# Order of the latent passes of a shared-key attention layer, the last row's store and second square, and the place of the conditioning sums in the heads

## The chip, the cores and the metric

The kernel runs on one core of a Trainium2 chip. The metric is the device time of one execution in microseconds, from the median of several runs. A profiled execution gives, beside its own time, the instructions of each engine in order of time: TensorE (PE, its weight loads PEld), VectorE (DVE), ScalarE (ACT), GpSimd (POOL) and SyncE (SP, which only issues transfers here; ScalarE issues some too).

## What is computed

A trunk of two layers over a sequence of 1024 rows of width 1024, float32. Layer 0 has a gated short convolution and a squared-ReLU MLP. Behind it, one shared key and value side is built from the residual stream, and layer 1 attends to it. This is the part that the change touches:

```python
def shared_kv(x, c_act, kv_ada_w, kv_ada_b, kv_norm_g, kv_a_w, kv_a_norm_g, kv_b_w, cos, sin):
    shift, scale = jnp.split(c_act @ kv_ada_w + kv_ada_b, 2, axis=-1)
    hkv = modulate(rmsnorm(x, kv_norm_g), shift, scale)
    kv_a = hkv @ kv_a_w                                    # 1024 x (256 + 64)
    c_kv = rmsnorm(kv_a[..., :KV_LORA], kv_a_norm_g)       # key latent, 256
    k_pe = apply_rope(kv_a[..., KV_LORA:], cos, sin)       # rotary key, 64
    kv = (c_kv @ kv_b_w).reshape(B, S, N_HEADS, QK_NOPE + V_HEAD)
    return kv[..., :QK_NOPE], kv[..., QK_NOPE:], k_pe

def mla_mixer(h, q_a_w, q_a_norm_g, q_b_w, o_w, k_nope, v, k_pe, cos, sin):
    q = (rmsnorm(h @ q_a_w, q_a_norm_g) @ q_b_w)           # query latent, 384; 8 heads of 128 + 64
    ...                                                    # scores, mask, softmax, values, output
```

The query side reads `h = modulate(rmsnorm(x, norm_g[1, 0]), ...)` with layer 1's own shift and scale ("1m"), the key side the same normalized rows with another shift and scale ("kv").

## The kernel before

Every float32 product is three matmuls (line 156): both operands are split into a high part and the rest (`hi`, `lo`), and low times high, high times low and high times high are summed in one PSUM bank. A high part is written by ScalarE or VectorE, a low part by VectorE (lines 159 and 160, 436 to 442). The sequence is held in two halves of 512 rows, "half 0" (row tiles 0 to 3) and "half 1" (row tiles 4 to 7).

`down_pairs` ends layer 0's MLP. Its last four row tiles go one after another: late products (L790), then `Seam.tile`, then `seam.front` of one step. `Seam.tile` adds the products, takes the sum of squares on ScalarE (`squares`, L271 and L273), scales and adds the row to the residual on VectorE (L327, L328), issues the row's store to `xs` from ScalarE (L329), and takes a second sum of squares, that of the new residual row. `Seam.flush` later turns it into the normalized row `y` (L278 on VectorE, L311 on ScalarE). The normalized rows are what the latents read.

A *step* of `h_steps` makes one of the eight column blocks of `h` for one half: four transposes on TensorE (L433) into a bank (`room`, mostly one of two `tp` banks), an eviction with scale and shift on ScalarE (L436, into one of two `tt` tiles), and on VectorE a cast for the high part (L441) and a subtraction for the low part (L442). Where `twice` is set, ScalarE writes the high part too. `front` issues a step's transposes and evictions, `back` the VectorE part.

The latents are eight passes over `h`, each pass 24 matmuls of 128x512 per 128 output columns. Before the change their order is: query latent of half 0 (three passes, `first_latents`; the third makes the columns of "1m", half 1), query of half 1 (the third makes "kv", half 0, in the place of "1m", half 0), key latent of half 0 (two passes; the second makes "kv", half 1), rotary key of half 0, key of half 1, rotary key of half 1. `latent` evicts each pass (L1193), squares it (L1194), sums (L1196), and then at once sums over partitions with a matmul by ones (L1197), takes the root (L1198), a reciprocal of 512 elements per partition (L1199), scales (L1201) and splits (L1202, L1203). The three query weight tiles are split once and kept for both halves; `up_split` has three buffers.

Heads 0 to 7 follow. Before the loop, head 0's query, rotary query and key are projected, half 1 first. Each head computes scores for row tiles 7 down to 0 and interleaves projections of the next head. `run_bg(5)` in each head does five steps of the conditioning sums (`ada_bc`, `ada_fm`; 34 steps in all, 24 of them a scaled sum on VectorE, nearly all on L186, with a 512 KB load each). Head 0 also makes the four value tiles, two after scores 7 and two after scores 6.

What sets the order: the instructions of a block inside `pinned()` keep their written order on each engine; all others are ordered by a planner that places an instruction where it expects its inputs and engine to be free. Transfers from SP go in the order that the planner gave. Buffers of a tag are reused as their last readers end, so a weight tile or a raw tile (four buffers) that is kept longer holds back a load.

Of the kernel before, what the change touches and what calls it, by code (L numbers as in the profile page):

```python
# [17 lines left out]
P = 128  # L18
D = 1024
S = 1024  # L20
KD = D // P
# [27 lines left out]
def trunk_kernel(ctx: ExitStack, tc: tile.TileContext, x, c, ada_w, ada_b, norm_g, conv_in_w, conv_w,  # L49
# [63 lines left out]
    def ld(out_, in_):  # L113
        nc.sync.dma_start(out_, in_)
# [169 lines left out]
    class Seam:  # L284
# [23 lines left out]
        def flush(self):  # L308
            if self.rest is not None:
                y, xr, ss = self.rest  # L310
                nc.scalar.activation(y, xr, AF.Copy, scale=rroot(ss))  # L311
            self.rest = None

        def tile(self, t, add, steps):
# [4 lines left out]
            with pinned():  # L319
# [251 lines left out]
    def first_latents(seam, steps, ws, h):  # L571

        ps_ = []
        for m, w in enumerate(ws):
            p_ = mm_ps() if m else big_ps()[:, :HALF]
            for k in range(KD):
                with pinned():
                    mm(p_, (w[0][:, k, :], w[1][:, k, :]), (h[0][:, k, :], h[1][:, k, :]), k == 0, k == KD - 1)
                    if m == 0 and k == 0:
                        seam.flush()  # L580
                    elif m == 2:
                        seam.back()
                        seam.front(steps, 1)
            ps_.append(p_)
# [73 lines left out]
    def down_pairs(ys, wd, before, seam, key=None, preps=()):  # L658
# [67 lines left out]
        with pinned([mybir.EngineType.SP]):  # L726
# [451 lines left out]
    firsts = first_latents(seam, h_steps(tp, ys, 1, "1m", hs[1]), ws, hs[0])  # L1178
# [4 lines left out]
    def latent(h, hf, ws, g, dst, steps=None, firsts=None):  # L1183
# [5 lines left out]
        rs = sqs[0]  # L1189
        sp = tp_ps()  # L1190
# [6 lines left out]
        nc.tensor.matmul(sp, ones, sqs[0], start=True, stop=True)  # L1197
        nc.scalar.activation(rs, sp, AF.Sqrt, scale=1.0 / (n * P), bias=eps_1)  # L1198
        nc.vector.reciprocal(rs, rs)  # L1199
        for m in range(n):  # L1200
            nc.vector.scalar_tensor_tensor(raws[m], raws[m], g[:, m:m + 1], rs, op0=ALU.mult, op1=ALU.mult)  # L1201
            nc.scalar.activation(dst[0][:, m, sl], raws[m], AF.Copy)  # L1202
            nc.vector.tensor_tensor(dst[1][:, m, sl], raws[m], dst[0][:, m, sl].bitcast(F32), op=ALU.subtract)  # L1203
# [28 lines left out]
    def rotary_keys(hf):  # L1232
        sl = slice(hf * HALF, (hf + 1) * HALF)
        z, y = halves(row_tile())
        rotated(up_mm(wk, hk[hf]), hf, 1.0, stab, z, y)
# [357 lines left out]
```

## Time and profile before

| | us |
|---|---|
| median of 3 runs | 2160.37 (2159.45 to 2161.99) |
| profiled execution, its own time | 2159.2 |
| its span, first to last instruction | 2157.4 |
| TensorE busy | 2062.0 (96%) |
| VectorE busy | 1541.2 (71%) |
| ScalarE busy | 1084.3 (50%) |

The mean granted TensorE clock is 0.991 of full speed. In the rows below, an instruction's row holds its start, its duration, engine and line, operation, output and input tiles, shapes, and in brackets how long its engine stood idle before it and what it waited for. A row of a stage holds its length, then the busy time and the number of instructions of PE, PEld, DVE, ACT and POOL, the granted clock, the share of the DMA engines and GB/s; where the view is of one line, only that line's engine is in it. A row of a group holds the count, total busy time and mean ns, and the idle time before it. Matmuls are pipelined, so the distance between starts, not the duration of one, tells their pace.

### The profile page before, as it was taken

What the parts mean: (1) busy time and instruction counts of PE and PEld (TensorE: products, weight loads), DVE (VectorE), ACT (ScalarE), POOL (GpSimd) and SP (SyncE); (2) the same over time, 40 slices, a digit from 0 to 9 for tenths busy, and PEclk for the clock granted to TensorE, in tenths of its full rate; (3) what the DMA queues carried; (4) which work ended last, traced back from release to release, by engine and by line L of the source; (5) the groups of instructions that cost most, each with busy time, mean ns of one, the idle gap of its engine ahead of it and who ended that gap; (6) DMA issues with size and microseconds to landing.
All of it is one profiled execution on the core that took longest, in us unless ns stands there. A gap on an engine that the chain in (4) does not pass through costs nothing.

```text
span 2157.4 us, 25064 instructions
## 1 busy us (share of the span) xinstructions
PE 2062.0 (96%) x9438; PEld 1688.2 (78%) x9438; DVE 1541.2 (71%) x2087; ACT 1084.3 (50%) x1533; POOL 5.3 (0%) x13
## 2 busy tenths in 40 slices
PE   4999999989999999999899999999899999999998
PEld 3788878768888788888677788887678888788886
DVE  6877876876665669977688887756875665566576
ACT  4533353745554444455665565555744444544443
POOL 0000000000000000000000000000000000000000
PEclk9999999999999999999999999999999999999999
DMA  7444464254553889656223331143254653774355
GB/s 223 121 138 147 137 205 133 88 184 161 182 181 139 280 292 322 208 166 211 69 70 120 97 96 35 59 135 138 71 185 150 215 180 134 266 252 158 98 175 167
DMA packets 251023, 344.47 MB, mean 160 GB/s; under 512 B 19253, under 2 KB 142482, under 8 KB 250902
## 3 DMA queue, kind: packets, MB, share of 16 engines
q1 hardware_dynamic: 208408, 252.50, 37.4%
q10 hardware_dynamic: 42494, 90.38, 11.3%
q8 instruction: 74, 1.21, 0.2%
q14 instruction: 47, 0.39, 0.1%
HBM read 258.94 MB, written 83.89 MB: 159 GB/s over the span
## 4 chain that ended last, share of the span: by engine, by line
PE 77%; DVE 11%; ACT 6%; DMA 3%; issue 2%; ACTq 0%; SPq 0%; DVEq 0%
PE one L156 42%; PE mm L156 20%; PE tp L156 7%; PE big L156 3%; PE big L1360 2%; ACT junk L271 2%; DVE y L327 1%; PE tp L1386 1%; DVE raw L328 1%; DMA aw<-in_ada_w_dram 1%; ACT slot L1210 1%; DVE av L909 1%; PE tp L433 1%; DVE ring L160 1%; DVE acc L186 1%
## 5 line engine op out<-in xcount | busy, mean ns | idle before, releaser
L156 PE MATMUL one<-slot,uphi 128*128 128x512 f32 x1224 | 377.8, 389 | 0.0
L156 PEld LDWEIGHTS one<-slot,uphi 128*128 128x128 f32 x1224 | 230.4, 188 | 48.3 <-issue 0.5
L156 PE MATMUL one<-ring,ring 128*128 128x512 f32 x1152 | 262.9, 389 | 2.3 <-DVE ring L160 2.3
L160 DVE TENSOR_TENSOR uplo<-raw,uphi 128x1024 fp32r<-128x1024 f32 x127 | 153.3, 1222 | 143.1 <-ACT uphi L159 143.1
L156 PEld LDWEIGHTS one<-ring,ring 128*128 128x128 f32 x1152 | 215.9, 188 | 48.3 <-ACT ring L159 3.1
L156 PE MATMUL one<-slot,uplo 128*128 128x512 f32 x612 | 240.7, 393 | 8.2 <-DVE y L528 3.8
L160 DVE TENSOR_TENSOR ring<-raw,ring 128x1024 fp32r<-128x1024 f32 x144 | 174.3, 1220 | 55.6 <-ACT ring L159 55.3
L159 ACT ACTIVATE ring<-raw 128x1024 fp32r<-128x1024 f32 x144 | 149.5, 1052 | 106.6 <-DMA raw<-ha 61.6
L159 ACT ACTIVATE uphi<-raw 128x1024 fp32r<-128x1024 f32 x127 | 134.7, 1061 | 118.6 <-PE one L156 82.3
L156 PE MATMUL mm<-ring,ring 128*128 128x512 f32 x768 | 185.0, 390 | 1.6 <-DVE ring L160 1.6
L156 PE MATMUL tp<-ring,ring 128*128 128x512 f32 x768 | 183.9, 389 | 0.0
L159 ACT ACTIVATE ring<-w 128x1024 fp32r<-128x1024 f32 x80 | 84.8, 1060 | 178.7 <-PE tp L156 102.7
L156 PEld LDWEIGHTS mm<-ring,ring 128*128 128x128 f32 x768 | 143.7, 188 | 32.1 <-DVE ring L160 2.5
L156 PEld LDWEIGHTS tp<-ring,ring 128*128 128x128 f32 x768 | 144.1, 188 | 29.9
L160 DVE TENSOR_TENSOR ring<-w,ring 128x1024 fp32r<-128x1024 f32 x80 | 97.8, 1222 | 81.1 <-ACT ring L159 81.1
L156 PEld LDWEIGHTS one<-slot,uplo 128*128 128x128 f32 x612 | 115.2, 188 | 35.8 <-DVE y L528 5.5
L186 DVE SCALAR_TENSOR_TENSOR acc<-raw,csil,acc 128x1024 f32<-128x1024 f32 x88 | 112.5, 1278 | 22.8 <-DMA raw<-in_ada_w_dram 18.0
L526 ACT ACTIVATE y<-one 128x512 f32<-128x512 f32 x66 | 39.0, 591 | 159.6 <-PE one L156 118.5
L156 PE MATMUL mm<-slot,uphi 128*128 128x512 f32 x344 | 109.2, 399 | 9.6 <-DVE slot L398 9.4
L156 PE MATMUL one<-slot,s 128*128 128x512 f32 x468 | 112.9, 390 | 1.1 <-DVE s L160 1.1
L156 PEld LDWEIGHTS one<-slot,s 128*128 128x128 f32 x468 | 87.6, 188 | 20.6 <-DVE s L160 2.4
L156 PE MATMUL one<-q,uphi 128*128 128x512 f32 x328 | 101.9, 392 | 0.0
(267 smaller groups left out, 3614.4 us busy)
## 6 DMA issues: line engine op xcount, KB each, us to landing
ha<-y ACTq DMA_DIRECT2D x224, 256.0 KB, 4.0
raw<-ha SPq DMA_DIRECT2D x112, 512.0 KB, 4.0
raw<-in_ada_w_dram SPq DMA_DIRECT2D x80, 512.0 KB, 4.3
raw<-in_mlp_up_w_dram SPq DMA_DIRECT2D x70, 512.0 KB, 4.5
w<-in_mlp_down_w_dram SPq DMA_DIRECT2D x48, 512.0 KB, 7.0
raw<-in_mlp_down_w_dram SPq DMA_DIRECT2D x32, 512.0 KB, 4.0
raw<-in_conv_in_w_dram SPq DMA_DIRECT2D x18, 512.0 KB, 4.1
xs<-raw ACTq DMA_DIRECT2D x18, 512.0 KB, 2.8
```

The costliest lines, as they stand in the source:

```text
L156: nc.tensor.matmul(out_, lhs[a], rhs[b], start=first and i == 0, stop=last and i == 2, skip_group_check=more)
L159: nc.scalar.activation(hi, src, AF.Copy)
L160: nc.vector.tensor_tensor(lo, src, hi.bitcast(F32), op=ALU.subtract)
L186: nc.vector.scalar_tensor_tensor(acc, raw, s, acc, op0=ALU.mult, op1=ALU.add)
L271: nc.scalar.activation(junk, src, AF.Square, accum_out=ss)
L327: nc.vector.scalar_tensor_tensor(y, y, rroot(ss), self.gmb, op0=ALU.mult, op1=ALU.mult)
L328: nc.vector.tensor_tensor(xr, xr, y, op=ALU.add)
L433: nc.tensor.transpose(p_[:, t * P:(t + 1) * P], ys[half * 4 + t][:, k * P:(k + 1) * P], ident)
L526: nc.scalar.activation(dst, x_, AF.Copy)
L909: nc.vector.scalar_tensor_tensor(acc, raw[:, i, :], csil[:, i:i + 1], acc, op0=ALU.mult, op1=ALU.add)
L1210: nc.scalar.activation(y[32 * i:32 * i + 32, :], p_[32 * j:32 * j + 32, :], AF.Copy, scale=scale)
L1360: nc.tensor.matmul(o_, a, m_, start=j == 0, stop=j == 4)
```

## The change

The diff does five things.

1. In the last row tiles of `down_pairs`, the step (transposes and evictions) is issued before the row's tile, not after it.
2. For the last row tile (`held`), the store and the second sum of squares are not issued in `Seam.tile` but in `flush`, which now stands in the third pass of the first latent, in the middle of its eight steps.
3. `first_latents`: its first pass reads the low parts of `h` two groups later than the high parts. Its third pass makes "kv", half 0.
4. The passes: query 0, key 0, rotary key 0 (makes "kv", half 1), key 1, rotary key 1 (makes "1m", half 1), query 1. `latent` returns its end (sum over partitions, root, reciprocal, scaling, split), which is called later. The query weights are loaded and split a second time for half 1. The sine table is held in a row tile.
5. Head 0: keys of both halves first, then query and rotary query of half 0, two value tiles, then query and rotary query of half 1; the other two value tiles follow scores 7 and 6. `run_bg(6)` in heads 1 to 7, none in head 0.

```diff
         def flush(self):
             if self.rest is not None:
-                y, xr, ss = self.rest
-                nc.scalar.activation(y, xr, AF.Copy, scale=rroot(ss))
+                y, xr, ss, held = self.rest
+                nc.scalar.activation(y, xr, AF.Copy, scale=rroot(ss or squares(self.nx, xr)))
+                if held is not None:
+                    nc.scalar.dma_start(self.xdst[held * P:(held + 1) * P, :], xr)
             self.rest = None
...
-                nc.scalar.dma_start(self.xdst[t * P:(t + 1) * P, :], xr)
+                if not held:
+                    nc.scalar.dma_start(self.xdst[t * P:(t + 1) * P, :], xr)
                 if not self.last:
-                    self.rest = (y, xr, squares(self.nx, xr))
+                    self.rest = (y, xr, None, t) if held else (y, xr, squares(self.nx, xr), None)
...
+            ps_.append(p_)
+            if m == 0:
+                jobs = []
+                for k in range(KD + LAG):
+                    jobs += [(1, 0, k), (0, 0, k)] * (k < KD) + [(0, 1, k - LAG)] * (k >= LAG)
+                with pinned():
+                    for i, (a, b, k) in enumerate(jobs):
+                        nc.tensor.matmul(p_, w[a][:, k, :], h[b][:, k, :], start=i == 0, stop=i == len(jobs) - 1)
+                    seam.back()
+                continue
             for k in range(KD):
                 with pinned():
                     mm(p_, (w[0][:, k, :], w[1][:, k, :]), (h[0][:, k, :], h[1][:, k, :]), k == 0, k == KD - 1)
-                    if m == 0 and k == 0:
-                        seam.flush()
-                    elif m == 2:
+                    if m == 2:
                         seam.back()
                         seam.front(steps, 1)
-            ps_.append(p_)
+                        if k == KD // 2:
+                            seam.flush()
...
-                    seam.tile(4 + t, lambda: done(t, banks_[t]), [])
                     with pinned():
+                        seam.back()
                         seam.front(steps, 1)
+                    seam.tile(4 + t, lambda: done(t, banks_[t]), [], t == 3 and bool(key))
...
-    firsts = first_latents(seam, h_steps(tp, ys, 1, "1m", hs[1]), ws, hs[0])
+    firsts = first_latents(seam, h_steps(tp, ys, 0, "kv", hs[0]), ws, hs[0])
...
-    latent(hs[0], 0, ws, gq, qaT, firsts=firsts)
-    steps = h_steps(tp, ys, 0, "kv", hk[0])
-    latent(hs[1], 1, ws, gq, qaT, steps)
+    end = latent(hs[0], 0, ws, gq, qaT, firsts=firsts)
     ws = [up_split(up, raw.rearrange("p (k m) -> p k m", k=KD)) for raw in raws_a]
+    end()
     wk = up_weights(up, [kv_a_w[:, KL:KL + ROPE]] * 2)
-    steps = h_steps(tp, ys, 1, "kv", hk[1])
-    latent(hk[0], 0, ws, gk, ckT, steps)
-    stab = raw_tile()
+    stab = row_tile()
     ld(stab, consts[:, C_T + S:])
+    end = latent(hk[0], 0, ws, gk, ckT)
+    p_ = up_mm(wk, hk[0], steps=h_steps(tp, ys, 1, "kv", hk[1]))
+    end()
+    rotary_keys(0, p_)
+    end = latent(hk[1], 1, ws, gk, ckT)
+    p_ = up_mm(wk, hk[1], steps=h_steps(tp, ys, 1, "1m", hs[1]))
+    ws = [up_weights(up, [w]) for w in cols_of(q_a_w[0], 3)]
+    end()
+    rotary_keys(1, p_)
     raw_kv, raw_q = load_kv_b(0), load_q_b(0)
-    rotary_keys(0)
-    latent(hk[1], 1, ws, gk, ckT)
+    kw = weights_in_rows(raw_kv.rearrange("p (k m) -> p k m", k=2))
     qw_ = weights_in_rows(raw_q[:, :768].rearrange("p (k m) -> p k m", k=3))
-    kw = weights_in_rows(raw_kv.rearrange("p (k m) -> p k m", k=2))
-    rotary_keys(1)
+    latent(hs[1], 1, ws, gq, qaT)()
...
     for hf in (1, 0):
+        keys(K, kw, 0, hf)
+    for hf in (0, 1):
         queries(Q, qw_, hf)
         rotary(R, qw_, hf, tp_ps)
-        keys(K, kw, 0, hf)
+        if hf == 0:
+            values(V, kw, 0)
+            values(V, kw, 1)
...
-        run_bg(5)
+        if h:
+            run_bg(6)
...
-            values(V, kw0, 0)
-            values(V, kw0, 1)
+            values(V, kw0, 2)
         end()
...
-            values(V, kw0, 2)
             values(V, kw0, 3)
```

More of the change, by code (lines that the diff above doesn't have):

```diff
@@ L309, in flush, with tile @@
             if self.rest is not None:
-                y, xr, ss = self.rest
-                nc.scalar.activation(y, xr, AF.Copy, scale=rroot(ss))
+                y, xr, ss, held = self.rest
+                nc.scalar.activation(y, xr, AF.Copy, scale=rroot(ss or squares(self.nx, xr)))
+                if held is not None:
+                    nc.scalar.dma_start(self.xdst[held * P:(held + 1) * P, :], xr)
             self.rest = None
-        def tile(self, t, add, steps):
+        def tile(self, t, add, steps, held=False):
             y = self.ys[t]
@@ L1196, in latent, with end @@
                 nc.vector.tensor_tensor(sqs[0], sqs[0], sqs[1], op=ALU.add)
[L1197 to L1203, printed above, removed]
+        def end():
+            rs, sp = sqs[0], tp_ps()
+            nc.tensor.matmul(sp, ones, sqs[0], start=True, stop=True)
+            nc.scalar.activation(rs, sp, AF.Sqrt, scale=1.0 / (n * P), bias=eps_1)
+            nc.vector.reciprocal(rs, rs)
+            for m in range(n):
+                nc.vector.scalar_tensor_tensor(raws[m], raws[m], g[:, m:m + 1], rs, op0=ALU.mult, op1=ALU.mult)
+                nc.scalar.activation(dst[0][:, m, sl], raws[m], AF.Copy)
+                nc.vector.tensor_tensor(dst[1][:, m, sl], raws[m], dst[0][:, m, sl].bitcast(F32), op=ALU.subtract)
+        return end
     def rotated(p_, hf, scale, stab, z, y):
```

6 lines of the change are left out of this document (2 added, 4 removed).

## The prediction

> **What bounds the kernel now.** I read the page first: share of the span by engine, then the chain that ended last.
>
> ```profile
> PE 2062.0 (96%) x9438; PEld 1688.2 (78%) x9438; DVE 1541.2 (71%) x2087; ACT 1084.3 (50%) x1533; POOL 5.3 (0%) x13
> PE 77%; DVE 11%; ACT 6%; DMA 3%; issue 2%; ACTq 0%; SPq 0%; DVEq 0%
> ```
>
> TensorE is busy 96% of 2157.4 us, so a change that adds and removes no matmul can only win TensorE's idle time, or the time of a lowered clock. The second view is therefore busy time by stage, over the stages that the diff touches: the first query product, the other latents, and head 0 in two parts.
>
> ```profile
> core 0: us, PE busy (x) PEld busy (x) DVE busy (x) ACT busy (x) POOL busy (x), PEclk, DMA share, GB/s
> 1027.00:1058.20 31.20, 23.14 (x110) 18.31 (x108) 18.45 (x31) 21.75 (x37) 0.00 (x0) 0.89 0.13 51
> 1058.20:1121.70 63.50, 61.74 (x290) 47.74 (x289) 52.97 (x70) 36.79 (x55) 0.00 (x0) 1.00 0.22 59
> 1121.70:1148.00 26.30, 22.90 (x118) 18.19 (x116) 25.14 (x36) 18.96 (x31) 0.95 (x1) 1.00 0.44 137
> 1148.00:1170.00 22.00, 20.44 (x111) 16.45 (x112) 19.52 (x44) 11.14 (x26) 0.00 (x0) 1.00 0.32 104
> ```
>
> Idle TensorE: 8.06, 1.76, 3.40 and 1.56 us, 14.8 in all. VectorE is idle 12.75 us of the first stage, and busy 44.66 of 48.3 us in the last two. The third view is TensorE's instructions in order of time through the first stage.
>
> ```profile
> 1027.75 0.39 PE L156 MATMUL big<-h,uplo 128*128 128x512 f32 x1
> ...
> 1031.83 0.39 PE L156 MATMUL big<-h,uplo 128*128 128x512 f32 x1
> ...
> 1034.03 0.50 PE L156 MATMUL big<-h,uplo 128*128 128x512 f32 x1 [1.36 <-ACT h L436]
> 1035.42 0.73 PE L156 MATMUL big<-h,uphi 128*128 128x512 f32 x2 [0.90 <-DVE h L442]
> 1036.00 0.39 PE L156 MATMUL mm<-h,uplo 128*128 128x512 f32 x1
> ...
> 1042.13 0.38 PE L433 MATMUL tp<-cs,y 128*128 128x128 f32 x2
> 1043.14 0.33 PE L433 MATMUL tp<-cs,y 128*128 128x128 f32 x1 [0.62 <-ACT y L311]
> 1048.65 0.48 PE L433 MATMUL tp<-cs,y 128*128 128x128 f32 x1 [5.19 <-ACT y L311]
> 1048.78 0.77 PE L156 MATMUL mm<-h,uplo 128*128 128x512 f32 x1
> ...
> 1052.49 0.48 PE L156 MATMUL mm<-h,uplo 128*128 128x512 f32 x1
> ...
> 1053.63 0.48 PE L156 MATMUL mm<-h,uplo 128*128 128x512 f32 x1
> ...
> 1058.16 0.47 PE L156 MATMUL mm<-h,uplo 128*128 128x512 f32 x1
> ...
> 1072.10 0.50 PE L156 MATMUL mm<-h,uplo 128*128 128x512 f32 x1 [1.63 <-ACT lat L1193]
> ```
>
> A block without waits first. From 1036.00 to 1042.13 run nine groups of three products, 0.681 us each. From 1053.63 to 1058.16 run four steps, a group and four transposes each: 1.133 us. The block from 1027.75 (16 groups, then 8 steps) would take 16 x 0.681 + 8 x 1.133 = 20.0 us. It took 30.4. The 10.4 us lost are three pieces.
>
> - The last h column: its group began one group after 1031.83, at 1032.5, and should have given way at 1033.2, not 1036.0: 2.8 us.
> - The transposes at 1042.13 read rows 4 to 7 and wait for the last normalized row: the next group should have come at 1042.6, not 1048.78: 6.2 us.
> - From 1048.78 to 1052.49 two steps took 3.7 us for 2.27: 1.4 us at a lowered clock, which the same stage in slices shows:
>
> ```profile
> 1046.00:1048.00 2.00, 0.00 (x0) 0.00 (x0) 0.57 (x2) 2.00 (x6) 0.00 (x0) 0.50 0.51 201
> 1050.00:1052.00 2.00, 2.00 (x8) 1.61 (x8) 1.09 (x2) 0.70 (x1) 0.00 (x0) 0.53 0.04 8
> ```
>
> **Part 1, the last h column: -2.8.** The last column's transposes ran at 1021.85, but ScalarE emptied them only at 1033.22, behind the squares and the scaled copy of the row's tile.
>
> ```profile
> 1021.85 0.60 PE L433 MATMUL one<-cs,y 128*128 128x128 f32 x4
> 1033.22 0.76 ACT L436 ACTIVATE h<-one,v,v 128x512 fp32r<-128x512 f32 x1
> ```
>
> The change issues transposes and evictions ahead of the row's tile, and the first product reads the low parts two groups later. The last low part should be there by about 1029, and is read near 1033. I take all 2.8; no cost is added, since the same two evictions only change places.
>
> **Part 2, which rows the transposes read: -6.2 and -1.4, +4.5.** The steps now take rows 0 to 3, ready long before, so both waits and the lowered clock go. What is late next is ScalarE, then VectorE, which are still finishing row 7:
>
> ```profile
> 1041.95 1.13 ACT L311 ACTIVATE y<-raw,small 128x1024 f32<-128x1024 f32 x1
> 1045.22 1.06 ACT L271 ACTIVATE junk<-raw 128x1024 bf16<-128x1024 f32 x1 [0.31 <-issue]
> 1047.46 1.14 ACT L311 ACTIVATE y<-raw,small 128x1024 f32<-128x1024 f32 x1
> 1043.59 1.23 DVE L328 TENSOR_TENSOR raw<-raw,y 128x1024 f32<-128x1024 f32 x1
> 1047.07 0.17 DVE L278 RECIPROCAL small<-small 128x1 f32<-128x1 f32 x1 [2.25 <-ACT small L273]
> L436 ACT ACTIVATE tt<-tp,v,v 128x512 f32<-128x512 f32 x24 | 18.6, 778 | 8.0 <-PE tp L433 7.0 <-DVE h L442 0.6 <-PE mm L156 0.3
> L441 DVE CAST h<-tt 128x512 fp32r<-128x512 f32 x24 | 10.2, 426 | 4.6 <-ACT tt L436 4.5
> L442 DVE TENSOR_TENSOR h<-tt,h 128x512 fp32r<-128x512 f32 x26 | 18.0, 692 | 6.1 <-ACT tt L436 5.3
> ```
>
> Two tp banks and two tt tiles make the loop. Without waits the third column would begin at 1038.65 (1027.75 + 16 x 0.681) + groups = 1041.6. By my chain ScalarE's copy of row 6 ends at 1042.7 (0.4 earlier than now), so the first eviction ends at 1043.4: **1.9** us of wait. VectorE ends row 7's sum at 1044.3; cast and subtraction take 0.426 + 0.692 a column, so the third eviction waits for a tt tile and the fifth transposes **0.65** us. Then the flush stands between the fifth and sixth eviction: square and root, reciprocal, scaled copy and store issue, which now run from 1045.22 to 1048.6 with two other evictions between (about 3 without them). The eighth transposes wait **2.65** us for it. Steps end at 1052.7 instead of 1047.7: 5.0. VectorE's casts queue behind the flush's reciprocal, and the first key product waits for them, but only at its eighth group, 4.8 us later, which covers it. The order of unpinned instructions is a planner's: it can lay key products into the last wait, leaving about 2.4, or lay two latent evictions (1.2) and a weight split (ScalarE 1.06, VectorE 1.18) into the loop, giving up to 8. I take 4.5, nearest to the chain; ends 2 and 8.
>
> The Trainium skill (TensorE: Matmul & The Clock Gate, Part 1) says that the clock halves after an idle window of about 3.4 us and needs about as long to return. The trace agrees after the 5.19 us wait (0.50, then 0.53). By it my three waits, each below 3.4, cost no clock, as in the sum; run together they would return 1.4. The same page (Architectural detail) calls ScalarE's and VectorE's queues strictly first in, first out, which speaks against a flush inside the loop: by it the third wait stays, and without it 2.65 us would go. The trace agrees, at 1033.22 above.
>
> **Part 3, the other latents: -1.6, +1.5.** The order becomes query 0, key 0, rotary 0 with steps, key 1, rotary 1 with steps, query 1. Same products and transposes; query 1's sum over partitions moves behind. The wait at 1072.10 was for an eviction held behind a weight split on ScalarE; with two products per latent between the steps it goes: 1.6 (0 if it recurs). Added are three loads and splits of q_a columns, kept until now:
>
> ```profile
> L160 DVE TENSOR_TENSOR uplo<-raw,uphi 128x1024 fp32r<-128x1024 f32 x3 | 3.5, 1182 | 0.3 <-ACT uphi L159 0.3
> L159 ACT ACTIVATE uphi<-raw 128x1024 fp32r<-128x1024 f32 x3 | 3.2, 1055 | 2.5 <-PE mm L156 2.5
> L1199 DVE RECIPROCAL sq<-sq 128x512 f32<-128x512 f32 x4 | 13.4, 3351 | 5.9 <-ACT sq L1198 5.9
> ```
>
> ScalarE's 3.2 us hide in its 26.7 idle us of that stage, and three more 512 KB loads in a DMA share of 0.22; SP queues them between the other weights. VectorE's 3.5 us find 10.5 idle us, fewer now, since the stage begins with its casts behind. Uncovered they cost 3.5. The first rotary weights wait for row 7's buffer, freed by the moved store: about 1054.4, then load, splits, 8 us: 1062.4, against a need at 1052.7 + 0.56 + 10.9 = 1064.2, two us of cover. The stepped stages want 8 x 1.118 = 8.9 us of VectorE in 8 x 1.133 = 9.1, so a backlog shows there: I take 1.5, ends 0 and 6.
>
> **Part 4, head 0: -0.5.** The conditioning sums leave it.
>
> ```profile
> 1120.00:1148.00 28.00, 6.33 (x5) 1.00 0.42 131
> 1148.00:1170.00 22.00, 3.75 (x3) 1.00 0.32 104
> 1170.00:1203.00 33.00, 32.60 (x170) 25.78 (x168) 28.96 (x55) 19.15 (x37) 0.00 (x0) 1.00 0.34 108
> 1081.07 0.59 ACT L1193 ACTIVATE raw<-mm 128x512 f32<-128x512 f32 x1
> 1093.59 0.69 DVE L1203 TENSOR_TENSOR qaT<-raw,qaT 128x512 fp32r<-128x512 f32 x1
> ```
>
> That is 10.1 us of VectorE out of a stretch where it sets the pace and TensorE idles 4.96 us. Against it: query 1 is now last, and its latent takes 13.2 us from eviction to last low part (1081.07 to 1094.28). Two keys (12 products), one query and rotary (18), and two values (24 half-width) cover 10.1; then query 1, its rotary part and their evictions follow before scores 7 can start, with only two values left to fill. I expect about 4.5 us idle where 4.96 stood: -0.5, between -3 (only the relief) and +5 (only the new chain). The sums land in heads 1 to 6 at six steps each; head 1 (1170 to 1203) has 4.0 us of VectorE idle with four sums in it already, and should they hold up a head, it is inside the +5.
>
> **Sum.** -2.8 - 6.2 - 1.4 + 4.5 - 1.6 + 1.5 - 0.5 = **-6.5 us**. The profiled execution took 2159.2 (span 2157.4 plus 1.8 around it), so 2152.7 on its footing; the median of the three runs is 2160.37, 1.2 higher, and I forecast on that: **2153.9**. All low ends give 2147.4 (-13.0), all high ends, with the 1.6 kept, 2168.9; both together are unlikely.
>
> **Rivals.**
>
> - *The stall only changes its place.* The flush costs the 8, the rotary weights and the chain of query 1 cost 2 more each: -10.4 + 8 - 1.6 + 2 + 1.5 = -0.5, **2159.9**, no change. For it: VectorE at 95% in head 0 and the late row 7. Against it: rows 0 to 3 need none of row 7. Chance 0.25; the change then does its reordering but not what it says.
> - *The planner fills nearly all waits.* Key products in the flush, scores or values in head 0: -10.4 + 2 - 1.6 + 0 - 3 = -13.0, **2147.4**. For it: now already evictions of later products stand between row 7's instructions on ScalarE. Against it: nothing else is ready at 1041.6. Chance 0.13.
> - *VectorE becomes the bound of the latents (slower).* If the latents' ends (a 3.35 us reciprocal, two or three scalings and subtractions, 6.2 to 7.6 us) stand ahead of the casts in both stepped rotary products, TensorE waits 7.6 + 6.2 us there, and each wait of over 5 us costs the 1.4 of clock: 16.6 in place of 1.5, so -6.5 + 15.1 = +8.6, **2169.0**. It turns the sign once these waits pass 8 us together. For it: stepped stages have 0.2 us of VectorE to spare. Against it: the same ends stood ahead of casts now, and TensorE idled only 1.76 in 63.5 us. Chance 0.08.
>
> **Chances.** The forecast holds 0.54, most of it faster. A measurement of this kernel tells about 0.2%, 4.3 us, from no change. Faster: 0.13 + 0.52 = 0.65; slower 0.08; within, 0.27. The range, 2147.5 to 2161.0, reaches from the filling planner to the stall that moved, and leaves out the slower case and half of the best one.
>
> **What would show it.** Right: no wait on ScalarE's h ahead of the first product's end; no 5 us wait and no clock below 1.0 in the first query product, but short waits of the transposes for evictions, the longest behind the flush; 4 to 5 us idle in head 0, now waiting for query 1. Wrong: a gap above 3 us in the steps, casts waiting behind a 3.35 us reciprocal, or a late rotary weight.

## The result: 0.27% slower

The changed kernel takes 2164.3 us (median of 16 runs, 2158.75 to 2172.14) against 2158.28 (16 runs, 2155.37 to 2161.99) of the kernel before on the same chip: 1.0027, with an interval from 1.0018 to 1.0037. The forecast was 2153.9, in a range up to 2161.0: 6.5 us faster than the 2160.37 known then, where 6.0 us slower was measured. The profiled execution takes 2162.63 us, span 2160.8, mean granted clock 0.989.

The busy times on the page of after:

```profile
PE 2063.7 (96%) x9438; PEld 1689.7 (78%) x9438; DVE 1544.4 (71%) x2090; ACT 1085.6 (50%) x1536; POOL 5.3 (0%) x13
```

TensorE does the same 9438 instructions. The next view of after, busy time by stage, has the first query product, the other latents, head 0 in two parts, and the later heads up to the last of the first projections' output evictions.

```profile
core 0: us, PE busy (x) PEld busy (x) DVE busy (x) ACT busy (x) POOL busy (x), PEclk, DMA share, GB/s
1024.54:1048.94 24.40, 21.77 (x103) 17.79 (x102) 18.04 (x29) 19.53 (x34) 0.00 (x0) 0.93 0.11 44
1048.94:1118.80 69.86, 63.99 (x289) 49.86 (x288) 53.58 (x74) 40.45 (x60) 0.00 (x0) 0.95 0.30 82
1118.80:1148.00 29.20, 26.66 (x134) 21.42 (x132) 25.96 (x34) 17.71 (x29) 0.95 (x1) 1.00 0.32 98
1148.00:1174.20 26.20, 19.51 (x96) 16.10 (x95) 21.24 (x44) 12.37 (x26) 0.00 (x0) 0.87 0.38 121
1174.20:1430.50 256.30, 248.73 (x1388) 206.87 (x1387) 196.72 (x401) 145.71 (x290) 0.00 (x0) 1.00 0.23 72
```

The stages of the two profiled executions, with their borders set at the same events (first product of the first latent; end of its third pass and eight steps; first product of head 0; its first output eviction; the last one). In after the eighth transposes come late, at 1051.68; there the border is the end of the third pass, 1048.50, plus the 0.44 us that these transposes take:

| us | before | after | difference | forecast |
|---|---|---|---|---|
| first query product | 30.4 | 24.4 | -6.0 | -5.9 |
| other latents | 63.55 | 69.87 | +6.3 | -0.1 |
| head 0 | 48.17 | 55.30 | +7.1 | -0.5 |
| later heads | 256.98 | 256.09 | -0.9 | 0 |

The sum is +6.5. The first latent itself starts at 1024.54 in after and at 1027.75 in before. That is no gain of the change: over the profiled executions below it starts between 1023.7 and 1029.7, with and without the change. The expected gain came in full, and two stages that were forecast at nothing gave it back twice.

Where the loss stands, by what TensorE waited for between 1024 and 1175 us in after (the three largest):

```profile
engine line waited for: us in total, times, longest us
PE big L1380 <- ACT p L1386: 6.7, 4, 3.2
PE mm L156 <- ACT lat L1204: 3.9, 1, 3.9
PE tp L436 <- ACT tt L439: 2.6, 1, 2.6
```

The third is the wait forecast in the steps. The first is in head 0, the second in the latents; neither has a term of that size in the forecast.

The same execution in slices that hold its lowered clock, three of the five:

```profile
1042.00:1044.00 2.00, 2.00 (x9) 1.61 (x8) 1.93 (x5) 1.93 (x4) 0.00 (x0) 0.52 0.05 12
...
1106.90:1110.30 3.40, 3.40 (x10) 2.62 (x9) 3.40 (x5) 2.42 (x4) 0.00 (x0) 0.50 0.01 2
...
1161.50:1164.90 3.40, 3.09 (x12) 2.99 (x13) 2.29 (x8) 1.27 (x5) 0.00 (x0) 0.51 0.29 110
```

Five spells of 3.4 us at half clock, each a loss of 1.7 us of work; the two left out begin at 1066.0 and 1151.3, behind the waits of 3.86 and 3.21 us. Before had one in these stages, the stretch of some 6.8 us to which the prediction's two slices belong. So of the latents' +6.3, 4.0 is idle time (63.55 us held 1.6 us of waits, 69.87 hold 5.6) and up to 3.4 the clock; of head 0's +7.1, 4.3 is idle (4.9 us of waits before, 9.2 after) and up to 3.4 the clock. The clock's share is up to a half of the loss, and each spell stands right behind a wait.

### The first query product, row by row

TensorE's instructions of after in order of time: the wait, then the end of the product.

```profile
1041.17 0.66 PE L436 MATMUL tp<-cs,y 128*128 128x128 f32 x4 [2.63 <-ACT tt L439]
...
1048.50 0.39 PE L156 MATMUL mm<-h,uplo 128*128 128x512 f32 x1
...
1051.68 0.60 PE L436 MATMUL tp<-cs,y 128*128 128x128 f32 x4
```

No row between 1024.54 and 1041.17 has a wait, so the last h column costs nothing now. The third transposes wait 2.63 us for a tt tile (1.9 in the forecast). The flush's wait is not there: from 1048.50 the planner has laid 14 matmuls of key 0 ahead of the eighth transposes. The forecast had that as its low case.

### The profile page after: what moved, and what is told of

Its sections match the earlier page's. It is cut to its first block, busy times and chain, and to the rows that moved or that the text cites. A ratio compares the mean times of both kernels' runs of the same rounds, so it can differ in the third digit from the quotient of the medians.

```text
span 2160.8 us, 25074 instructions
## 1 busy us (share of the span) xinstructions
PE 2063.7 (96%) x9438; PEld 1689.7 (78%) x9438; DVE 1544.4 (71%) x2090; ACT 1085.6 (50%) x1536; POOL 5.3 (0%) x13
## 3 DMA queue, kind: packets, MB, share of 16 engines
q8 instruction: 74, 1.21, 0.2%
## 4 chain that ended last, share of the span: by engine, by line
PE 77%; DVE 12%; ACT 6%; DMA 2%; issue 2%; ACTq 0%; SPq 0%; DVEq 0%
PE one L156 42%; PE mm L156 20%; PE tp L156 7%; PE big L156 3%; PE big L1380 3%; ACT junk L271 1%; PE tp L1406 1%; DVE y L329 1%; DVE raw L330 1%; ACT slot L1226 1%; DVE uplo L160 1%; DMA aw<-in_ada_w_dram 1%; DMA raw<-hd 1%; DVE ring L160 1%; DVE av L922 1%
```

## The experiments

In all of them the whole computation is done; e8 adds matmuls that nothing reads. Each ratio is to the kernel before on the same chip. One table for all, stages by the borders above (the first two rows of that table together as "latents"); a total is a median, a stage is of one profiled execution. That one is above the median in e6 (2164.7), e12 (2161.5) and e13 (2161.8), and one spell of half clock more or less moves a stage by 1.7 us:

| kernel | latents | head 0 | later heads | total | ratio (interval) |
|---|---|---|---|---|---|
| before | 93.96 | 48.17 | 256.98 | 2158.3 | |
| after | 94.27 | 55.30 | 256.09 | 2164.3 | 1.0027 (1.0018 to 1.0037) |
| e1, after: all sums held | 94.28 | 48.66 | 279.13 | 2179.0 | 1.0095 (1.0072 to 1.0117) |
| e2, after: own latent tiles | 88.61 | 55.02 | 257.21 | 2160.0 | 1.0006 (0.9996 to 1.0015) |
| e3, before: all sums held | 95.19 | 44.49 | 281.41 | 2178.7 | 1.0090 (1.0075 to 1.0106) |
| e4, before: step ahead of the row | 94.31 | 48.14 | 256.75 | 2157.3 | 0.9994 (0.9984 to 1.0003) |
| e5, after: first sum held | 94.33 | 48.67 | 261.05 | 2163.0 | 1.0024 (1.0014 to 1.0034) |
| e6, before: first sum held | 94.07 | 44.52 | 264.10 | 2159.1 | 1.0001 (0.9991 to 1.0010) |
| e7, e2 and e5 together | 88.66 | 48.93 | 261.83 | 2156.9 | 0.9998 (0.9989 to 1.0007) |
| e8, after: the wait filled | 94.39 | 55.01 | 256.13 | 2164.6 (one run) | |
| e9, after: sums written as before | 92.54 | 55.66 | 255.96 | 2163.5 | 1.0029 (1.0020 to 1.0038) |
| e10, e2: values and sums as before | 88.23 | 55.62 | 259.14 | 2160.3 | 1.0016 (1.0007 to 1.0026) |
| e11, query 1 as third latent | 91.38 | 50.45 | 257.44 | 2155.6 | 0.9993 (0.9984 to 1.0003) |
| e12, e10 with first sum held | 88.19 | 51.49 | 262.86 | 2158.3 | 1.0004 (0.9995 to 1.0013) |
| e13, e11 with first sum held | 91.32 | 46.67 | 262.60 | 2158.0 | 1.0002 (0.9992 to 1.0011) |

### The latents: one pair of tiles for all ends

The end of one latent keeps its columns in a tile `lat` and their squares in a tile `sq`, each with one buffer that all latents share. The rows of after around the 3.86 us wait, VectorE, then ScalarE, then TensorE:

```profile
1056.45 3.35 DVE L1213 RECIPROCAL sq<-sq 128x512 f32<-128x512 f32 x1 [1.45 <-ACT sq L1212]
...
1060.79 1.40 DVE L1215 SCALAR_TENSOR_TENSOR lat<-lat,vecs,sq 128x512 f32<-128x512 f32 x2
...
1062.78 1.29 DVE L1217 TENSOR_TENSOR qaT<-lat,qaT 128x512 fp32r<-128x512 f32 x2
...
1064.16 1.08 ACT L1204 ACTIVATE lat<-mm 128x512 f32<-128x512 f32 x2 [0.64 <-DVE qaT L1217]
1064.81 0.50 PE L156 MATMUL mm<-h,uplo 128*128 128x512 f32 x1 [3.86 <-ACT lat L1204]
```

Read from below: TensorE stands at the first group of rotary key 0 and needs a bank that ScalarE empties at 1064.16, with key 0's two passes in it. ScalarE may not write `lat` before VectorE's last reading of query 0's columns, whose end (root, reciprocal, scaling, split) has run since query 0's third pass was evicted. That eviction in after and, below, in before, with before's rows around the wait at 1072.10:

```profile
1050.85 0.59 ACT L1204 ACTIVATE raw<-mm 128x512 f32<-128x512 f32 x1
```

```profile
1058.04 0.59 ACT L1193 ACTIVATE raw<-mm 128x512 f32<-128x512 f32 x1
...
1069.36 1.29 DVE L1203 TENSOR_TENSOR qaT<-lat,qaT 128x512 fp32r<-128x512 f32 x2
1070.51 1.06 ACT L159 ACTIVATE uphi<-raw 128x1024 fp32r<-128x1024 f32 x1 [0.40 <-PE mm L156]
1071.47 1.07 ACT L1193 ACTIVATE lat<-mm 128x512 f32<-128x512 f32 x2
```

In before, too, `lat` came free only at 1070.65, 0.8 us ahead of the eviction; the split in between cost no more than that. In before the third pass is evicted as its product ends. In after it is evicted 2.35 us behind that end (1048.50), since the flush and the last evictions of the steps stand ahead of it on ScalarE. The wait is 3.86 - 1.63 = 2.23 us longer. So the flush that TensorE didn't wait for in the steps is paid one product later; this is read from the rows, and e8 below agrees.

e2 gives the two key latents tiles of their own.

```diff
-        raws = halves_of(ad.tile([P, D], F32, tag="gmb", name=nm("lat"), bufs=1), *([raw_tile()] if n > 2 else []))
-        sqs = halves_of(ad.tile([P, D], F32, tag="acc", name=nm("sq"), bufs=1))
+        if n > 2:
+            raws = halves_of(ad.tile([P, D], F32, tag="gmb", name=nm("lat"), bufs=1), raw_tile())
+            sqs = halves_of(ad.tile([P, D], F32, tag="acc", name=nm("sq"), bufs=1))
+        else:
+            raws, sqs = halves_of(row_tile()), halves_of(row_tile())
```

> The changed kernel, with tiles of their own for the two key latents (evicted values and squares), where all latents share one pair. Theory A (the 3.86 us wait ahead of the first rotary product is the key latent's eviction waiting for the query latent's last scaling, which still holds the shared tiles, and the half clock behind it follows from the wait): the stage of the other latents, 66.8 us, falls by 4 to 5.5, the whole time as well. Theory B (VectorE is full there, and the wait would only move to the next cast or weight split): the stage falls by less than 2.

The latents fall from 94.27 to 88.61 us, a little more than theory A's 5.5, and the total by 4.3. The three added weight splits are still there, so they aren't what cost the latents their time. The first group of rotary key 0 in e2, without a wait, and the stretch behind it, at full clock:

```profile
1066.12 0.50 PE L156 MATMUL mm<-h,uplo 128*128 128x512 f32 x1
```

```profile
1066.00:1070.00 4.00, 4.00 (x23) 3.21 (x23) 4.00 (x8) 3.81 (x7) 0.00 (x0) 1.00 0.49 137
```

Of the 5.6 us of waits 2.8 are left, 0.60, 0.69 and a new one of 1.54 for VectorE's rotation, and both spells of half clock are gone. One spell can also be missing by itself: in e9, whose latents are those of after, the same waits stand, but the last pair has no spell behind it (why, is in the last section), and the latents take 92.54. So the shared tiles are the cause of 4 to 5.7 of the latents' 6.3.

The other two waits of after stand behind the end of key 1, whose reciprocal is laid ahead of the last step's subtraction:

```profile
1100.34 3.34 DVE L1213 RECIPROCAL sq<-sq 128x512 f32<-128x512 f32 x1
1103.61 0.62 DVE L445 TENSOR_TENSOR h<-tt,h 128x512 fp32r<-128x512 f32 x1
...
1104.29 0.73 PE L156 MATMUL mm<-h,uphi 128*128 128x512 f32 x2 [0.58 <-DVE h L445]
...
1106.21 0.50 PE L156 MATMUL mm<-h,uplo 128*128 128x512 f32 x1 [1.19 <-DVE y L1227]
```

This is the mechanism of the slower rival. It is there, at 1.8 us of waits and a spell of half clock behind them, not at the 13.8 us that the rival needed.

### The sums: they don't leave head 0

Line 186 alone in the time of head 0, in before:

```profile
1118.00:1174.00 56.00, 10.08 (x8) 1.00 0.38 122
```

and in after:

```profile
1118.00:1174.00 56.00, 10.15 (x8) 0.94 0.35 107
```

Eight sums in both. Head 0 issues none any more, but nothing binds those of head 1 to their place: the planner finds them ready and VectorE free, and pulls them forward. This could be seen before the change: the source wrote five steps into head 0, and the eight sums above stand there. In after they stand in front of the reductions that the softmax of the first scores waits for (VectorE, then ScalarE, then TensorE):

```profile
1144.69 2.59 DVE L186 SCALAR_TENSOR_TENSOR acc<-raw,csil,acc 128x1024 f32<-128x1024 f32 x2
...
1147.32 1.28 DVE L186 SCALAR_TENSOR_TENSOR acc<-raw,csil,acc 128x1024 f32<-128x1024 f32 x1
1148.52 1.22 DVE L1383 TENSOR_REDUCE small<-big 128x1 f32<-128x1024 f32 x1
...
1153.58 1.07 DVE L1383 TENSOR_REDUCE small<-big 128x1 f32<-128x896 f32 x1
1148.96 1.28 ACT L1386 ACT_TABLE_LOAD   x1
1150.25 1.11 ACT L1386 ACTIVATE p<-big,small 128x1024 f32<-128x1024 f32 x1
...
1154.68 1.01 ACT L1386 ACTIVATE p<-big,small 128x896 f32<-128x896 f32 x1 [3.23 <-DVE small L1383]
1151.51 0.79 PE L1380 MATMUL big<-kk,r 128*128 128x512 f32 x1 [3.21 <-ACT p L1386]
```

Three sums, 3.87 us, stand ahead of the first reduction, which ends at 1149.74. ScalarE, which has put another eviction and its table load first, starts the exponent at 1150.25, and TensorE waits 3.21 us for it; in e5 below, without the sums, that wait is 0.67. The second exponent waits 3.23 us for its reduction, with two more sums ahead of it.

e9 undoes the edit of the sums alone, e1 and e3 pin every sum to its written place on VectorE (in after and in before), and e5 and e6 pin only the first, so that the others, which need it, cannot come earlier:

```diff
# e9
-        if h:
-            run_bg(6)
+        run_bg(5)
# e1 (e3: the same on before, whose run_bg(5) becomes run_bg(6))
         if h:
-            run_bg(6)
+            with pinned([mybir.EngineType.DVE]):
+                run_bg(6)
# e5 (e6: the same on before)
+        if h == 1:
+            with pinned([mybir.EngineType.DVE]):
+                run_bg(2)
         if h:
-            run_bg(6)
+            run_bg(4 if h == 1 else 6)
```

> The changed kernel, with the conditioning sums written as before (five steps in every head, head 0 too). Theory A (the edit of the sums does nothing: the planner pulls head 1's sums into head 0 wherever they are written): head 0's stage is within 1.5 us of 55.3, the whole time within 2 us of the changed kernel. Theory B (the edit takes work off head 0, or made it worse): the stage moves by more than 2.

> The changed kernel, with the conditioning sums of heads 1 to 6 tied on VectorE to their head, so that the planner can't lay them into head 0. Theory A (the sums were still in head 0, in front of the reductions of scores 7 and 6, and that made the waits for the exponentials and two spells of half clock): the stage from the end of the query passes to head 0's first output, 55.4 us in the changed kernel, falls to 46 to 49, and the whole time by 5 to 8 us. Theory B (the new order of head 0 has used up the values that filled those waits; the sums don't matter): the stage stays within 2 us of 55.4 and the whole time within 2 us.

> The kernel before, with only one thing changed: no conditioning sums in head 0, six steps in each later head and tied to it on VectorE. Theory A (in head 0 VectorE sets the pace, and eight sums, 10.1 us, lie there): the stretch from the end of the rotary pass to head 0's first output, 48.3 us with 4.96 us of TensorE idle, falls by 2 to 4 us; later heads lose less than 1. Theory B (the sums only fill VectorE's gaps there, and are paid in the later heads): the stretch falls by less than 1, or the later heads lose what it wins; the whole time within 1 us.

> The changed kernel, with only the first conditioning sum tied to head 1 on VectorE; the others follow it in their chain and the planner spreads them. Theory A (head 0 loses 6.6 us to sums pulled into it, and the 20 us that the later heads lost with all sums tied come from sums standing in a row, not from moving them): head 0's stage, 55.3 us, comes to 48 to 50 as with all sums tied, the later heads stay within 2.5 us of their 256.1, and the whole time falls by 4 to 7 us against the changed kernel. Theory B (the later heads have no room for eight more sums): they lose what head 0 wins, and the whole time stays within 2 us of the changed kernel.

> The kernel before, with the sums starting in head 1 and only the first tied to it. Theory A: head 0's stretch, 48.2 us, comes to 44.5 as with all sums tied, the later heads to 257 to 259, the whole time falls by 2 to 3.5 us. Theory B: the later heads lose what head 0 wins; within 1 us.

e9: head 0 55.66 against 55.30, total 2163.5 against 2164.3. The edit of the sums does nothing by itself. e5: with no sum in head 0, it takes 48.67, 6.6 less, and the same step takes 3.7 from before (e6: 44.52). In head 0 the waits for exponents fall from 6.7 to 2.4 us. So the sums do cost head 0 its time, and more in the new order. But the later heads pay it back: +5.0 in e5, +7.1 in e6, and the totals move by -1.3 and +1.1, which the intervals don't tell from nothing (e6 against the 2158.0 of the kernel before in its own batch). That is theory B on the time of both, though head 0 did what theory A said. The two sizes are rough: e5's later heads hold one spell of half clock where after has none, e6's three where before has one. e1 and e3 show how dear a firm place is: head 0 falls as theory A had it, but the later heads take 23 and 24 us more, and e1's total, which was to fall by 5 to 8 us, rises by 14.7.

e7 puts e2 and e5 together:

> The changed kernel, with both mends: own tiles for the key latents, and the first conditioning sum tied to head 1. Theory A (the two losses lie in different stages and add): latents and query product about 88.6 us, head 0 48 to 50, the whole time 9 to 12 us below the changed kernel and 3 to 5 below the kernel before. Theory B (one of the gains is only passed on to the next stage): no more than 6 below the changed kernel, not clearly below the kernel before.

The two gains add up in the stages (88.66 and 48.93). The total, 2156.9, is 7.4 below the changed kernel and 0.9998 of before; that is between the theories (9 to 12, and no more than 6), since the later heads take 5.7 us more. The loss against before is gone with two small repairs; a gain is not shown.

### Head 0: the sums or query 1's chain?

Without sums, head 0 still takes 4.2 us more in the new order (48.67 in e5, 44.52 in e6), of which the later heads give 3.0 back. e10 puts the values back behind the scores, e12 is e10 with the first sum held, e11 moves query 1 ahead of key 1 (its third pass makes "kv", half 1) with head 0 as before the change, and e13 is e11 with the first sum held.

```diff
# e10: e2, and
-        if hf == 0:
-            values(V, kw, 0)
-            values(V, kw, 1)
...
-        if h:
-            run_bg(6)
+        run_bg(5)
...
-            values(V, kw0, 2)
+            values(V, kw0, 0)
+            values(V, kw0, 1)
...
+            values(V, kw0, 2)
# e11: e2, head 0 as before, and
-    p_ = up_mm(wk, hk[0], steps=h_steps(tp, ys, 1, "kv", hk[1]))
+    p_ = up_mm(wk, hk[0], steps=h_steps(tp, ys, 1, "1m", hs[1]))
...
+    end = latent(hs[1], 1, ws, gq, qaT, h_steps(tp, ys, 1, "kv", hk[1]))
+    ws = [up_weights(up, [w]) for w in cols_of(kv_a_w, 2)]
...
+    end = latent(hk[1], 1, ws, gk, ckT)
+    p_ = up_mm(wk, hk[1])
```

> The changed kernel with own tiles for the key latents (2160.0), the value tiles as before (two behind scores 7, two behind scores 6) and the sums as before. Theory A (the order costs head 0 its fillers: with the values used up, TensorE has nothing to lay into the waits for the exponentials): head 0's stage, 55.0 us, falls by 3 to 5, the whole time too. Theory B (it is the chain of query 1, which has to end before scores 7 to 4 can start; the values only fill another wait): head 0's stage falls by less than 1.5, or rises, since queries 1 then wait uncovered.

> A version of its own: first query product as changed, own tiles for the key latents, but query 1 ahead of key 1 (order: query 0, key 0, rotary 0, query 1, key 1, rotary 1), with three more weight splits, and head 0, its values and the sums exactly as before. Theory A (the first product's 6 us are real, and what ate them was the shared tiles and query 1 standing last): latents and query product take 88 to 91 us against 94.0 before, head 0 48 to 49 as before, the whole time 3 to 6 us below the kernel before. Theory B (VectorE is full in the latents, and three more splits cost what the order wins): the latents take 93 or more, and the time is no better than before.

> The kernel of e10 (own tiles for the key latents, all values behind the scores), with the sums out of head 0 as in e5: the first one tied to its place in head 1. In e10 head 0 took 55.6 us with a wait of 5.5 us for query 1's rotary part, and four sums of 1.28 us stood between query 1's scalings and that part on VectorE. Theory A (the sums in front of query 1's chain are the loss): the wait for the rotary part falls below 1.5 us, head 0 takes 46 to 49.5 us, the clock stays above 0.98 there, the later heads take 4 to 8 us more than the 256.1 of after, and the total is 2155 to 2158. Theory B (query 1's chain is late by itself): the wait stays above 3.5 us, head 0 takes 52 us or more, and the total is 2159 or more.

> The kernel of e11 (query 1 as the third latent, head 0 as before the change), with the sums out of head 0 as in e5. In e11 head 0 took 50.5 us and the later heads 257.4. Theory A (with query 1 early no chain waits behind the sums, so that moving them only moves their cost, as from before to e6): head 0 takes 45 to 47.5 us, the later heads 262 to 265, and the total is within 1.5 us of e11's, 2155 to 2158. Theory B (the sums cost less in the later heads than in head 0): the later heads take 257 to 260 and the total is 2150 to 2154, faster than both kernels.

e10 leaves head 0 at 55.62, as theory B had it, but the wait has another name. TensorE, then VectorE, in e10:

```profile
1141.01 0.80 PE L1383 MATMUL big<-kk,r 128*128 128x512 f32 x1 [5.47 <-DVE r L1353]
1132.01 1.28 DVE L186 SCALAR_TENSOR_TENSOR acc<-raw,csil,acc 128x1024 f32<-128x1024 f32 x1
...
1138.95 1.28 DVE L186 SCALAR_TENSOR_TENSOR acc<-raw,csil,acc 128x1024 f32<-128x1024 f32 x1
1140.27 1.40 DVE L1353 TENSOR_TENSOR r<-slot,r 64x512 fp32r<-64x512 f32 x2
```

Scores 7 now wait for query 1's rotary part, with four sums in its way from 1132.01 on, the first and the last of which are shown. In e12 they are gone, and so is that wait, but a new one comes at the values, whose evictions stand behind query 1's chain on both engines:

```profile
1136.86 4.00 PE L156 MATMUL mm<-w,ckT 128*128 128x256 f32 x17 [3.30 <-DVE v L1367]
```

Head 0 takes 51.49 in e12, between the two theories' bounds: the sums in front of the chain cost 4.1 of it. e11 has query 1 early and the sums where they were: head 0 takes 50.45, and no wait there is above 1.11 us. It falls short of theory A all the same, in head 0 (48 to 49), in the total (1.8 below the 2157.4 of before on its chip, not 3 to 6) and by a little in the latents, 91.38: a wait of 2.73 us for a sum of squares at 1097.67 is new, with half clock behind it. e13 takes the sums out of e11: 46.67, and the later heads +5.2. Its total is 2.4 above e11's (1.9 by the ratios), more than theory A allowed, but the two intervals overlap; theory B's gain isn't there. Without sums, then, head 0 takes 4.8 less with query 1 early (46.67) than with it last (51.49); the order inside head 0 goes with it and has no run of its own.

So it takes both for the whole loss, query 1 late and VectorE full: of the 7.1, 0.5 is left without the sums (e5) and 2.3 with query 1 early (e11). How it splits between them can't be given as two numbers, since taking the sums away adds to the later heads, and moving query 1 adds to the latents.

e11 has the lowest median, 2155.6. Its interval reaches 1.0003, so it isn't shown to beat the kernel before; it does beat the changed one, whose interval begins at 1.0018.

### The first product: which of its waits count

e4 makes edit 1 and edit 3's first pass alone, with the flush behind that pass, in the kernel before, with the rows and passes as they were.

```diff
# the first pass as in the change, then seam.flush(), and
...
+                    with pinned():
+                        seam.back()
+                        seam.front(steps, 1)
                     seam.tile(4 + t, lambda: done(t, banks_[t]), [])
-                    with pinned():
-                        seam.front(steps, 1)
```

> The kernel before, with only the step issued ahead of the row's tile and the low parts read two groups later in the first pass; the transposes still read rows 4 to 7. Theory A (the wait for the last column and the wait for the last row are one chain on ScalarE and VectorE, which ends with the last normalized row): the 2.26 us wait goes, the wait for the last row grows by nearly as much, and the first query product takes 29.5 to 30.5 us as now (30.4). Theory B (the two waits add, as the prediction's sum has them): it takes 27.6, and the whole time falls by 2.8.

The latents take 94.31 against 93.96, the total 0.9994 of before: nothing measurable, as theory A had it. TensorE's rows in e4:

```profile
1039.76 0.45 PE L433 MATMUL tp<-cs,y 128*128 128x128 f32 x1 [2.90 <-ACT y L311]
1045.55 0.48 PE L433 MATMUL tp<-cs,y 128*128 128x128 f32 x1 [5.34 <-ACT y L311]
```

The 2.26 us of waits saved at the last column come back as longer waits for the normalized rows, 8.2 us in all against 5.8. The two losses are one chain in a row; only with rows 0 to 3 for the transposes is the first one worth anything.

e8 fills the 2.63 us wait with ten matmuls that nothing reads.

```diff
+            if k == 2:
+                d_, wv = big_ps()[:, :HALF], w[0].rearrange("p k m -> p (k m)")[:, :HALF]
+                for _ in range(10):
+                    nc.tensor.matmul(d_, w[0][:, 0, :], wv, start=True, stop=True)
```

> The changed kernel, with ten more matmuls (2.3 us), whose result nothing reads, laid into the wait of the third transposes in the first query product. Theory A (the half clock that follows is caused by that wait of 2.6 us, though it is shorter than the clock's window): no half clock in the next 4 us, and the first query product ends about 1.6 us earlier. Theory B (a wait this short does not lower the clock; the spell has another cause, such as the load before it): the half clock stays, and the product ends no earlier.

TensorE's rows in e8, and the slice behind them:

```profile
1040.13 2.45 PE L596 MATMUL big<-uphi 128*128 128x512 f32 x10
1042.93 0.66 PE L436 MATMUL tp<-cs,y 128*128 128x128 f32 x4 [0.35 <-ACT tt L439]
```

```profile
1042.00:1048.00 6.00, 5.65 (x33) 4.26 (x32) 5.87 (x10) 5.16 (x10) 0.00 (x0) 1.00 0.54 138
```

The clock stays at 1.00 where it was 0.52, so the wait was the half clock's cause (theory A). One execution would be thin; but of the ten others with this wait eight have half clock behind it, and in e10 and e12, the two without, the clock's grid cuts the wait in two (last section). The last transposes come 27.67 us after the start, against 27.14 in after: ScalarE is busy 5.16 of these 6 us, and its flush sets the pace (theory B on the time). What TensorE wins in the steps it waits out up to rotary key 0: 1.29 us in key 0's products and 2.67 behind them, where after has 3.86. So this spell of half clock cost nothing, since another engine set the pace (latents 94.39 against 94.27).

## Why the prediction was wrong

- **Parts 1 and 2** were right in the mechanism, and by some luck in the number: -6.0 measured, -5.9 forecast. Of the new waits, 5.0 forecast and 4.5 taken, one of 2.63 came, and up to 1.7 of half clock, which was forecast not to come. The flush was hidden as the low case had it, but only in this stage: its time is in part 3's wait. That -2.8 and -6.2 were two terms was wrong in detail, as e4 shows; together they are the 9.0 that was counted, once the transposes read rows 0 to 3.
- **Part 3 is the first step that failed.** It said of the wait at 1072.10 that with two products per latent between the steps "it goes". The row named `lat`, and I read the eviction as held behind a weight split on ScalarE. The split was at most 0.8 us of it; what the runs show is the reuse of one buffer, in which the end of query 0 and the next latent's passes meet whichever latent is next. The wait came back as 3.86 us, longer by the flush that I had counted in the steps, and with half clock behind it. The term was +6.3 for -0.1, and e2 takes 4 to 5.7 of it away with two tiles. The range had allowed "0 if it recurs", not that it grows.
- **Part 4 is the second.** It took "the conditioning sums leave it" from the diff. The prediction says itself that unpinned instructions are the planner's; by that, sums that are ready stay wherever VectorE has a gap, and eight of eight did. Its own rows (x5 and x3) show eight sums where the source wrote five steps. Without the -3 of relief the part was left with its "only the new chain", +5, and +7.1 came, since the planner's sums now stood in front of a reduction or of query 1's chain, and two waits brought half clock.
- **The lowered clock** was given no price for waits below 3.4 us, after the Trainium skill (TensorE: Matmul & The Clock Gate, Part 1). In the runs an idle time of 2.0 us within one window of 3.41 us was enough each time. Four such spells in the latents' and head 0's waits are up to 6.8 of the 13.4 us lost there.
- **The rivals.** The slower one named one of the two stages and the right sign with another mechanism, and had 0.08. The first rival's "VectorE at 95%" holds for the first of head 0's two rows; both together give 92%. That the change would not do what it says for the sums was mentioned under no rival, though the planner's freedom was known.
- **The tests named** would have caught it: a gap above 3 us did appear, at the first group of the stepped rotary product, and the waits of head 0 were 9.2 us, not 4 to 5, most of them for a softmax.

## What to carry to other kernels

Before a stage is moved next to another of its kind, look up which scratch tiles both use and how many buffers these have: the row that names the tile of a waiting eviction is the hint, and a second buffer may be worth more than the new order. In a kernel whose order a planner makes, a statement moved to a later place moves nothing unless a dependence holds it there; and work that must be done somewhere on a nearly full engine is paid for elsewhere, so an edit's worth is the sum over both places. Two stalls in a row on one chain are not two gains.

## What the hardware showed beyond the forecast

The granted clock halved behind waits well below 3.4 us, the length of one spell: 2.63, 3.21, 0.58 with 1.19, and 0.86 with 2.15 us in after, beside the 3.86. Shorter ones, such as the 1.63 us at 1072.10 in before, left it at 1.00. In between it isn't the length alone: both kernels have the same wait of 2.00 us in a later head, with half clock behind it in before and full clock in after.

What decides is mostly the place of the wait. Within an execution all changes of the granted clock lie on one grid of 3.41 us: the five spells of after begin at 1042.07, 1065.96, 1106.92, 1151.30 and 1161.54, which are 7, 12, 13 and 3 times 3.413 us apart. TensorE in windows of this grid around the 2.00 us wait, in before:

```profile
1400.05:1403.46 3.41, 1.78 (x9) 1.00 0.14 34
1403.46:1406.88 3.42, 3.06 (x12) 0.50 0.31 120
```

and in after:

```profile
1403.88:1407.30 3.42, 2.21 (x12) 1.00 0.04 10
1407.30:1410.71 3.41, 2.50 (x16) 1.00 0.38 144
```

Each row ends with TensorE's busy time and matmuls, the granted clock, the DMA share and GB/s. In before 1.63 us of idle time lie in one window, and the next one runs at half clock. In after the grid cuts the wait, 1.21 and 0.91 us, and the clock stays at 1.00. Over the 15 executions, from 100 to 2140 us, a window at full clock with 2.0 us or more idle is followed by half clock 63 times of 63, one with less than 1.2 us never, in 8621; in between, 37 times of 129, and what decides there is open. The Trainium skill (TensorE: Matmul & The Clock Gate, Part 1) calls the window free-running. The runs agree: the same 2.63 us wait falls on different places of the grid from execution to execution. For a forecast, a wait of 2 to 4 us is to be priced at its length plus up to 1.7 us, where TensorE is the bound.
